# Small matmuls of four token mixers regrouped by array tile: RWKV scores, solved blocks and samples, HGRN2 outputs, attention heads in pairs

## The chip, the cores and the metric

The kernel runs on one core of a Trainium2 chip. The metric is the device time of one execution in microseconds (us). TensorE (PE in the profile) multiplies, VectorE (DVE), ScalarE (ACT) and GpSimd (POOL) do the elementwise work, SyncE (SP) issues most transfers. Each engine works through an instruction list of its own, whose order is fixed when the program is built.

## The reference, cut to what matters

Two layers of a decoder trunk in float32, on 288 token columns: a prompt of 256 tokens and 8 samples of 4 tokens each. A layer is

```python
u = RMSNorm(x); cols = u @ W_in            # 1024 wide, projections of four mixers and four gate blocks
o_A = RG-LRU(...)                          # convolution, gates, linear recurrence
o_B = RWKV-7(...)                          # 4 heads of 64, matrix state
o_C = HGRN2(...)                           # 4 heads, 128 features a head, values of 64
o_D = attention(...)                       # 4 heads of 64, dilated windows, 1024 cached positions for samples
x += W_o(sum_n sigmoid(G_n) * (o_n @ P_n))
x += W_down(gelu(conv3(v @ W_gate)) * (v @ W_up)),  v = RMSNorm(x)
```

The parts that the change touches are these. RWKV-7 steps a state `s = s*w + (s a) b' + v k'` and reads `s r`; HGRN2 sums `att = q k exp(decay)` within and between chunks of 64 and multiplies by the values; the attention takes a softmax of masked scores and multiplies by the values.

## The kernel before, in words

Features lie on partitions, tokens on columns. Two kinds of matmul share TensorE.

**The stream.** Every large weight is fetched in chunks of 512 KB (`chunk`, L320), split by ACT and DVE into two float32r parts `h` and `l`, and multiplied with the split activations (`prod`, L330): three products of 128x288 per 128x128 block of weights. These are the rows `pm<-tp,h`, `pm<-tp,l`, `pm<-y,h` and so on. `unit` (L1374) queues nine of them and then calls `mix`.

**The mixers.** Each mixer is a generator: RG-LRU (`branch_a`), RWKV (`branch_b`, L521), HGRN2 (`branch_c`, L914, two instances of a head pair each) and the attention (`branch_d`, L1135). `mix` (L1356) lets the mixers whose gap (`GAP`, L140) has passed go on by one `yield`, at most four of them in a slot. The small matmuls that they queue thus stand between the stream's products. `ORDER` (L147) sets the order of projections and gates. What stands in the program in this way is then put into one list per engine by a scheduler.

Small products are mostly float32 (a float32 product leaves two records in the trace, so x16 of them is 8 products; a streamed float32r product leaves one). A product may use part of the 128x128 array: 64 contracted rows in either row half, 64 or 32 output columns in a column half or quarter. "Tile" below is such a part, written rows x columns.

PSUM has three sets of banks (`BANKS`, L138): 3 `pm` for the stream, 2 `xb` for RWKV (and the attention's samples), 3 `xc` for HGRN2 and the attention. A name such as `xb<-b,kb` is out<-in.

The places that the change touches:

- `scores(h, a, q)` in RWKV (L730): for one head parity h (row half h) the four 128x128 score blocks of two head pairs and two chunks, into one `xb` bank. It is called eight times a layer: for `ab` (L737) and for the three matrices of `zz` (L814).
- `samples()` in RWKV (L625): the samples' small problem, with heads stacked on partitions in quarters.
- The loop over two chunks (L828 to 883): the solved product `u = X rr` (with `Y` a 64x64 tile and `Z` a 128x64 tile), the new state, and the outputs.
- HGRN2's outputs (L1067 to 1075): per head five products, of 64-row and 128-row tiles by turns.
- The attention's prompt heads (L1289 to 1327): scores, softmax, three transposes, three products with the values, one head after another.

## Time and profile before

| | us |
|---|---|
| time, median of 3 runs | 1227.33 (1226.59 to 1227.88) |
| the profiled execution: span | 1226.4 |
| TensorE busy in it | 1191.4 (97%) |
| VectorE busy | 854.3 (70%) |
| ScalarE busy | 612.2 (50%) |
| GpSimd busy | 551.5 (45%) |

The profiled execution's own time is shown as its span alone; the page has no other figure for it, and the span lies 0.9 us under the median of the runs. A row of the timeline gives the start of a run of like records, its length to the last modelled end, and the engine, line, operation, names, tile (rows*columns of the array), output and count. Matmuls overlap, so the distance from a start to the next start is what a run takes from the engine. Idle time before a run stands in brackets with what ended it. The windows give busy time per engine in a stretch of the span, and `PEclk`, the clock that TensorE was granted (1.00 is 2.4 GHz, 0.50 is 1.2 GHz).

### The profile page before, as it was taken

What the parts mean: (1) busy time and instruction counts of PE and PEld (TensorE: products, weight loads), DVE (VectorE), ACT (ScalarE), POOL (GpSimd) and SP (SyncE); (2) the same over time, 40 slices, a digit from 0 to 9 for tenths busy, and PEclk for the clock granted to TensorE, in tenths of its full rate; (3) what the DMA queues carried; (4) which work ended last, traced back from release to release, by engine and by line L of the source; (5) the groups of instructions that cost most, each with busy time, mean ns of one, the idle gap of its engine ahead of it and who ended that gap; (6) DMA issues with size and microseconds to landing.
All of it is one profiled execution on the core that took longest, in us unless ns stands there. A gap on an engine that the chain in (4) does not pass through costs nothing.

```text
span 1226.4 us, 26434 instructions
## 1 busy us (share of the span) xinstructions
PE 1191.4 (97%) x10596; PEld 1118.1 (91%) x10596; DVE 854.3 (70%) x1383; ACT 612.2 (50%) x1044; POOL 551.5 (45%) x862
## 2 busy tenths in 40 slices
PE   7988999999999999999998999999999999999997
PEld 6987788997899999999998978899889999999997
DVE  7897757576468888875568887575655878888543
ACT  5776446454345444443367844464543454444432
POOL 3745537240335666642228337352312636656322
PEclk9998999999999999999998989999999999999999
DMA  7344137248545555555543432543665455555552
GB/s 253 126 133 140 53 122 249 87 141 293 188 155 166 175 167 170 160 177 169 161 161 123 139 104 86 190 166 104 210 244 194 145 160 173 166 166 161 180 164 82
DMA packets 64042, 196.33 MB, mean 160 GB/s; under 512 B 8416, under 2 KB 12640, under 8 KB 63920
## 3 DMA queue, kind: packets, MB, share of 16 engines
q1 hardware_dynamic: 61872, 189.56, 47.1%
q0 software_dynamic: 1328, 4.33, 1.1%
q8 instruction: 83, 1.36, 0.4%
q10 hardware_dynamic: 720, 0.76, 0.2%
q14 instruction: 39, 0.32, 0.1%
HBM read 187.08 MB, written 6.49 MB: 158 GB/s over the span
## 4 chain that ended last, share of the span: by engine, by line
PE 83%; DVE 6%; POOL 4%; ACT 2%; issue 2%; DMA 2%; SPq 0%; DVEq 0%; ACTq 0%; POOLq 0%
PE pm L179 48%; PE xc L179 26%; PE xb L179 8%; POOL b L193 1%; DVE l L193 1%; DMA c<-in_vc 1%; POOL a L193 1%; DVE c L193 1%; DMA w<-in_w 1%; PE xc L182 1%; DVE c L956 1%; DVE c L202 1%; POOL b L200 1%; DVE b L196 0%; ACT h L185 0%
## 5 line engine op out<-in xcount | busy, mean ns | idle before, releaser
L179 PE MATMUL pm<-tp,h 128*128 128x288 f32 x2880 | 606.4, 302 | 5.9 <-DVE a L193 3.8
L185 ACT ACTIVATE h<-w 128x1024 fp32r<-128x1024 f32 x299 | 316.1, 1059 | 398.3 <-issue 211.9
L179 PEld LDWEIGHTS pm<-tp,h 128*128 128x128 f32 x2880 | 471.5, 191 | 16.7 <-ACT c L185 4.2
L193 DVE TENSOR_TENSOR l<-w,h 128x1024 fp32r<-128x1024 f32 x299 | 383.4, 1282 | 112.5 <-ACT h L185 111.3
L179 PE MATMUL pm<-tp,l 128*128 128x288 f32 x1440 | 431.8, 300 | 2.5 <-DVE l L193 2.5
L179 PEld LDWEIGHTS pm<-tp,l 128*128 128x128 f32 x1440 | 275.2, 191 | 7.6 <-DVE l L193 4.0
L179 PE MATMUL xc<-tp,h 128*128 128x288 f32 x896 | 183.9, 296 | 1.6 <-ACT tp L185 0.9
L179 PEld LDWEIGHTS xc<-tp,h 128*128 128x128 f32 x896 | 144.7, 188 | 3.3 <-ACT tp L185 1.3
L179 PE MATMUL xc<-tp,l 128*128 128x288 f32 x448 | 132.3, 295 | 0.0
L193 POOL TENSOR_TENSOR tmp<-a,rs 128x256 f32<-128x256 f32 x96 | 74.9, 800 | 72.5 <-ACT a L185 72.5
L193 POOL TENSOR_TENSOR tp<-tp,th 128x288 f32<-128x288 f32 x48 | 50.1, 1060 | 105.5 <-DVE th L196 105.5
L196 DVE SCALAR_TENSOR_TENSOR a<-a,pv,a 128x304 f32<-128x304 f32 (+2 forms) x112 | 84.2, 752 | 7.2 <-ACT a L185 5.5
L179 PEld LDWEIGHTS xc<-tp,l 128*128 128x128 f32 x448 | 84.3, 188 | 0.4 <-DVE l L193 0.4
L193 POOL TENSOR_TENSOR tmp<-x 128x288 f32<-128x288 f32 x28 | 28.3, 1009 | 108.0 <-DVE x L193 107.7
L193 DVE TENSOR_TENSOR th<-pm,rs 128x288 f32<-128x288 f32 x64 | 29.1, 455 | 60.9 <-PE pm L179 60.5
L193 POOL TENSOR_TENSOR c<-c 128x512 f32<-128x512 f32 (+2 forms) x32 | 37.2, 1178 | 47.1 <-PE xc L179 41.4
L193 DVE TENSOR_TENSOR tmp<-pm,tmp 128x288 f32<-128x288 f32 x48 | 22.0, 458 | 39.1 <-POOL tmp L193 39.0
L185 ACT ACT_TABLE_LOAD x34 | 43.6, 1283 | 0.6
L179 PE MATMUL pm<-y,h 128*128 128x288 f32 x192 | 41.1, 302 | 0.0
L185 ACT ACTIVATE c<-c 128x256 f32<-128x256 f32 (+2 forms) x68 | 30.7, 499 | 16.0 <-POOL c L193 15.1
L185 ACT ACTIVATE a<-a 128x304 f32<-128x304 f32 (+2 forms) x76 | 33.8, 446 | 9.9 <-DVE a L196 6.6
L193 DVE TENSOR_TENSOR c<-c,c 128x256 f32<-128x256 f32 (+2 forms) x56 | 34.9, 660 | 3.5 <-ACT c L185 3.3
(304 smaller groups left out, 1922.7 us busy)
## 6 DMA issues: line engine op xcount, KB each, us to landing
w<-in_wf SPq DMA_DIRECT2D x96, 512.0 KB, 3.6
w<-in_wg SPq DMA_DIRECT2D x64, 512.0 KB, 3.8
w<-in_w SPq DMA_DIRECT2D x59, 512.0 KB, 3.5
w<-in_wd SPq DMA_DIRECT2D x48, 512.0 KB, 3.5
c<-in_kc SPq DMA_DIRECT2D x32, 320.0 KB, 5.7
c<-in_vc SPq DMA_DIRECT2D x32, 320.0 KB, 5.0
w<-in_wb SPq DMA_DIRECT2D x16, 512.0 KB, 3.7
w<-in_wo SPq DMA_DIRECT2D x16, 512.0 KB, 3.5
```

Source lines behind the costliest of these rows:

```text
L179: nc.tensor.matmul(o, a, b, start=start, stop=stop)
L182: nc.tensor.transpose(o, i, ident)
L185: S.activation(o, i, f, **kw)
L193: e.tensor_tensor(o, a, b, op)
L196: V.scalar_tensor_tensor(o, a, s, b, op0, op1)
L200: (e or V).tensor_scalar(o, a, s1, None, op0)
L202: (e or V).tensor_scalar(o, a, s1, s2, op0, op1)
L956: V.tensor_tensor_scan(pr(b, h), C("crst", 0, 256), pr(f, h), 0.0, MUL, ADD)
```

## The change

The order in which the mixers' small products are queued is altered, and some of them are put on other tiles. The arithmetic is the same sum in another grouping.

- **RWKV scores.** `scores(a, q)` fills the banks of both head parities at once, the parity being the innermost loop. `ab` and the three matrices of `zz` are taken from such pairs.
- **RWKV samples.** The products for `b` and `k` over head pairs get a bank and a place of their own. The products with the cached state take `at` and `rt` directly, four products of a 64x32 tile each, in place of two of a 64x64 tile on a gathered copy. The addition of `sar` to `rr` is done by DVE in place of four products with the identity. The output products are grouped by operand, and all lie on 32x64 tiles.
- **RWKV solved blocks.** `Y` gets zeros in its lower half (a GpSimd memset), and the product of the upper blocks uses all 128 rows. State and output products are queued with the head innermost.
- **HGRN2 outputs.** `ato` holds the diagonal and the cross block of a 128-token chunk (with zeros in the third quadrant), so that a head has three products of N=128 on 128x64 tiles; the two heads of a pair alternate.
- **Attention.** Prompt heads are taken in pairs: both heads' scores, both softmaxes, six transposes, six products with the values, the heads alternating.
- **RWKV's small rank products.** `pa` is queued right behind `pw`.

The core of the diff (comments that the new file drops are left out):

```diff
+            pw, pa = X("xb")[:, :N], X("xb")[:, :N]
+            first = mm(pw, lora[0:64, 0, f], wa[0:64])
+            with tc.issue_after(first.ins):
+                mm(pa, lora[64:128, 0, f], wa[64:128])
...
-            p, pk = X("xb"), X("xb")
+            p = X("xb")
             for n, (a, q) in enumerate(((bt, at), (kt, at), (bt, rt), (kt, rt))):
                 for h in range(4):
                     mm(p[hr(h), n * NS:(n + 1) * NS], a[h // 2][rows(h), sc], q[h // 2][rows(h), sc])
             for h in range(4):
-                i, z = h // 2, 64 * (h % 2)
-                one = ident[rows(h), rows(h)]
-                mm(p[hr(h), P:P + 64], v[i][rows(h), sc], one)
-                mm(pk[z:z + NS, i * 64:i * 64 + 64], bt[i][rows(h), sc], one)
-                mm(pk[z + NS:z + 64, i * 64:i * 64 + 64], kt[i][rows(h), sc], one)
+                mm(p[hr(h), P:P + 64], v[h // 2][rows(h), sc], ident[rows(h), rows(h)])
             yield
...
-            act(stk[:, :P], pk[:, :P], AF.Copy)
             vh = stk[:, P:192]
             act(vh, p[:, P:192], AF.Copy)
+            p = X("xb")
+            for h in range(4):
+                i, z = h // 2, 64 * (h % 2)
+                one = ident[rows(h), rows(h)]
+                mm(p[z:z + NS, i * 64:i * 64 + 64], bt[i][rows(h), sc], one)
+                mm(p[z + NS:z + 64, i * 64:i * 64 + 64], kt[i][rows(h), sc], one)
+            act(stk[:, :P], p[:, :P], AF.Copy)
...
-            ar = R([P, 2, 2, NS], "sm")
-            for i in range(2):
-                G.tensor_copy(ar[:, i, 0], at[i][:, sc])
-                G.tensor_copy(ar[:, i, 1], rt[i][:, sc])
             sar = []
-            for i in range(2):
+            for src in (at, rt):
                 p = X("xb")
-                for z in range(2):
-                    mm(p[rows(z)], ar[rows(z), i].rearrange("p w t -> p (w t)"), s0[i][rows(z)].rearrange("p b v -> p (b v)"))
+                for h in range(4):
+                    mm(p[hr(h)], src[h // 2][rows(h), sc], s0[h // 2][rows(h)].rearrange("p b v -> p (b v)"))
...
             for h in range(4):
-                z = 64 * (h % 2)
-                mm(p[hr(h), :64], zs[hr(h), 0], vh[hr(h)], start=True, stop=False)
-                mm(p[hr(h), :64], ident[rows(h), z:z + NS], sar[h // 2][rows(h)], start=False, stop=True)
+                mm(p[hr(h), :64], zs[hr(h), 0], vh[hr(h)])
...
-            act(rr, p[:, :64], AF.Copy)
+            tt(V, rr, p[:, :64], sar[0], ADD)
...
-            ps_ = [X("xb"), X("xb")]
-            for h in range(4):
-                o = ps_[h // 2][rows(h), :NS]
-                mm(o, u[hr(h)], zs[hr(h), 1], start=True, stop=False)
-                mm(o, vh[hr(h)], zs[hr(h), 2], start=False, stop=False)
-                z = 64 * (h % 2) + NS
-                mm(o, sar[h // 2][rows(h)], ident[rows(h), z:z + NS], start=False, stop=True)
-            yield
             for i in range(2):
-                act(py[i][:, sc], ps_[i][:, :NS], AF.Copy)
+                p = X("xb")
+                for n, a in enumerate((vh, sar[1], u)):
+                    for h in (2 * i, 2 * i + 1):
+                        b = (zs[hr(h), 2], ident[hr(h), hr(h)], zs[hr(h), 1])[n]
+                        mm(p[rows(h), :NS], a[hr(h)], b, start=n == 0, stop=n == 2)
+                act(py[i][:, sc], p[:, :NS], AF.Copy)
+            yield
...
-        def scores(h, a, q):
-            p = X("xb")
+        def scores(a, q):
+            ps_ = [X("xb"), X("xb")]
             for i in range(2):
                 for c in range(2):
                     z, s = 2 * i + c, slice(c * P, c * P + P)
-                    mm(p[:, z * P:(z + 1) * P], a[i][rows(h), s], q[i][rows(h), s])
-            return p.rearrange("p (a b) -> p a b", a=4)
+                    for h in range(2):
+                        mm(ps_[h][:, z * P:(z + 1) * P], a[i][rows(h), s], q[i][rows(h), s])
+            return [p.rearrange("p (a b) -> p a b", a=4) for p in ps_]
         ab, abo = (R([P, 8, 64], "kb") for _ in range(2))
-        for h in range(2):
-            p, o = scores(h, bt, at), slice(4 * h, 4 * h + 4)
-            yield
+        sab = scores(bt, at)
+        yield
+        for h, p in enumerate(sab):
+            o = slice(4 * h, 4 * h + 4)
             for r in (0, 64):
                 act(ab[r:r + 32, o], p[r:r + 32, :, r:r + 64], AF.Copy)
                 act(ab[r + 32:r + 64, o, 0:32], p[r + 32:r + 64, :, r + 32:r + 64], AF.Copy)
             act(abo[0:64, o], p[0:64, :, 64:128], AF.Copy)
...
+        G.memset(Y[64:128], 0.0)
+        zz = [[], []]
+        for a, q, mk in ((kt, at, "us"), (bt, rt, "ui"), (kt, rt, "ui")):
+            pair = scores(a, q)
+            yield
+            for h, p in enumerate(pair):
                 z = R([P, 4, P], "kb")
                 G.memset(z, 0.0)
-                p = scores(h, a, q)
-                yield
                 V.copy_predicated(z, Mn(mk, 4), p)
-                row.append(z)
-            zz.append(row)
+                zz[h].append(z)
...
-                    mm(p[0:64, o], Y[0:64, z], rr[0:64, o])
+                    mm(p[0:64, o], Y[:, z], rr[:, o])
                     mm(p[64:128, o], Z[:, z], rr[:, o])
...
-                for h in range(2):
-                    o, tc_ = p[rows(h), i * 64:i * 64 + 64], slice(c * P + 64 * h, c * P + 64 * h + 64)
-                    mm(o, tk[i][0][:, tc_], u[:, i, hc(h)], start=True, stop=False)
-                    mm(o, tk[i][1][:, tc_], tk[i][2][:, tc_], start=False, stop=True)
-            yield
+                for m in (1, 0):
+                    for h in range(2):
+                        o, tc_ = p[rows(h), i * 64:i * 64 + 64], slice(c * P + 64 * h, c * P + 64 * h + 64)
+                        mm(o, tk[i][m][:, tc_], tk[i][2][:, tc_] if m else u[:, i, hc(h)], start=m == 1, stop=m == 0)
+            yield
...
-                for h in range(2):
-                    o, tc_ = p[rows(h), i * P:(i + 1) * P], slice(c * P + 64 * h, c * P + 64 * h + 64)
-                    mm(o, u[:, i, hc(h)], zz[h][1][:, 2 * i + c], start=c == 0, stop=False)
-                    mm(o, tk[i][2][:, tc_], zz[h][2][:, 2 * i + c], start=False, stop=True)
+                for m in (2, 1):
+                    for h in range(2):
+                        o, tc_ = p[rows(h), i * P:(i + 1) * P], slice(c * P + 64 * h, c * P + 64 * h + 64)
+                        mm(o, tk[i][2][:, tc_] if m == 2 else u[:, i, hc(h)], zz[h][m][:, 2 * i + c],
+                           start=c == 0 and m == 2, stop=m == 1)
             yield
...
-        ato = R([P, 4, 64], "kc")
-        act(ato[0:64], p[0:64, :256].rearrange("p (z m) -> p z m", z=4), AF.Copy)
-        G.tensor_copy(ato[64:128], att[64:128])
+        ato = R([P, 4, P], "kc")
+        G.memset(ato[64:128, :, 0:64], 0.0)
+        G.tensor_copy(ato[0:64, :, 0:64], att[0:64])
+        G.tensor_copy(ato[64:128, :, 64:P], att[64:128])
+        act(ato[0:64, :, 64:P], p[0:64, :256].rearrange("p (z m) -> p z m", z=4), AF.Copy)
...
-        for h in range(2):
-            r = rows(h)
-            v0, v1 = vt[:, h * 64:(h + 1) * 64], vt[:, P + h * 64:P + (h + 1) * 64]
-            mm(p[r, 0:64], v0[0:64], att[0:64, h])
-            mm(p[r, 64:P], v0, ato[:, h])
-            mm(p[r, P:TP], v0, a01[:, h], start=True, stop=False)
-            mm(p[r, P:P + 64], v1[0:64], att[0:64, 2 + h], start=False, stop=False)
-            mm(p[r, P + 64:TP], v1, ato[:, 2 + h], start=False, stop=True)
+        for o_, c, m, start, stop in ((0, 0, ato, True, True), (P, 0, a01, True, False), (P, 1, ato, False, True)):
+            for h in range(2):
+                mm(p[rows(h), o_:o_ + P], vt[:, c * P + h * 64:c * P + (h + 1) * 64], m[:, 2 * c + h], start=start, stop=stop)
...
-        def scores(h):
-            p, i = X("xc")[:, :384], h // 2
+        def scores(i):
+            ps_ = [X("xc")[:, :384] for _ in range(2)]
             for lo, q0, w in ((0, 0, P), (P, P, TP)):
-                mm(p[:, lo:lo + w], qs[rows(h), i, q0:q0 + P], ks_[rows(h), i, :w])
-            return p
+                for z, p in enumerate(ps_):
+                    mm(p[:, lo:lo + w], qs[rows(z), i, q0:q0 + P], ks_[rows(z), i, :w])
+            return ps_
...
-        e = softmax(p)
-        for h in range(4):
-            if h < 3:
-                p = scores(h + 1)
-            yield
-            pe = X("xc")
-            for n in range(3):
-                tr(pe[:, n * P:(n + 1) * P], e[:, n])
-            yield
-            t = R([P, 3, P], "kc")
-            act(fl(t), pe[:, :384], AF.Copy)
-            if h < 3:
-                e = softmax(p)
-            yield
-            hc = slice(64 * h, 64 * h + 64)
-            mm(y[rows(h), h // 2, 0:P], vt[0][:, hc], t[:, 0])
-            mm(y[rows(h), h // 2, P:TP], vt[0][:, hc], t[:, 1], start=True, stop=False)
-            mm(y[rows(h), h // 2, P:TP], vt[1][:, hc], t[:, 2], start=False, stop=True)
+        for i in range(2):
+            es = [softmax(q_) for q_ in p]
+            yield
+            pes = [X("xc") for _ in range(2)]
+            for e, pe in zip(es, pes):
+                for n in range(3):
+                    tr(pe[:, n * P:(n + 1) * P], e[:, n])
+            yield
+            ts_ = []
+            for pe in pes:
+                ts_.append(R([P, 3, P], "kc"))
+                act(fl(ts_[-1]), pe[:, :384], AF.Copy)
+            if i == 0:
+                p = scores(1)
+            yield
+            for o_, c, n in ((0, 0, 0), (P, 0, 1), (P, 1, 2)):
+                for z, t in enumerate(ts_):
+                    mm(y[rows(z), i, o_:o_ + P], vt[c][:, (2 * i + z) * 64:(2 * i + z + 1) * 64], t[:, n],
+                       start=n < 2, stop=n != 1)
```

Three places show what the scheduler made of it, all on PE in the first layer.

HGRN2's outputs, first head of pair 0, before, behind the products of the pair's state. `kc_1860` is `att`, `kc_2325` and `kc_2360` are `ato` and `a01` (each name is the operand that streams; the values are `a_2399`); a row reads out<-moving,held. The other head's last four and the second pair's ten follow in the same manner.

```order
L179 MATMUL xb_1561<-b_1170,kb_1029 32x32 x32
L179 MATMUL xc_2457<-a_2413,kc_2455 128x64 x4
L179 MATMUL xc_2465<-kc_1860,a_2399 64x64
L179 MATMUL xc_2465<-kc_2325,a_2399 64x64
L179 MATMUL xc_2465<-kc_2360,a_2399 64x128
L179 MATMUL xc_2465<-kc_1860,a_2399 64x64
L179 MATMUL xc_2465<-kc_2325,a_2399 64x64
L179 MATMUL xc_2465<-kc_1860,a_2399 64x64
```

The same head pair and then the other one, after:

```order
L179 MATMUL xb_1591<-kb_1589,b_1123 32x32 x32
L179 MATMUL xc_2493<-a_2446,kc_2491 128x64 x4
L179 MATMUL xc_2501<-kc_2351,a_2432 64x128 x2
L179 MATMUL xc_2501<-kc_2390,a_2432 64x128 x2
L179 MATMUL xc_2501<-kc_2351,a_2432 64x128 x2
L179 MATMUL xc_2520<-kc_2380,a_2446 64x128 x2
L179 MATMUL xc_2520<-kc_2421,a_2446 64x128 x2
L179 MATMUL xc_2520<-kc_2380,a_2446 64x128
L179 MATMUL xb_1643<-b_1124,kb_1029 32x32 x32
L179 MATMUL xc_2520<-kc_2380,a_2446 64x128
```

A head's five products, which go from a 64x64 to a 128x64 tile and back, became three on a 128x64 tile, the pair's two heads in two column halves (x2). Eleven of the twelve products of both pairs now stand in a row, and the last behind 32 products of RWKV's doubling.

RWKV's scores for two of the `zz` matrices, before (`xb_2218` and `xb_2304` are the banks of two matrices of the same parity, row half 0):

```order
L179 MATMUL pm_2992<-tp_101,l_2996 128x288
L179 MATMUL xb_2218<-b_912,b_910 128x128 x2
L179 MATMUL xb_2218<-b_975,b_973 128x128 x2
L179 MATMUL xb_2304<-b_912,b_913 128x128 x2
L179 MATMUL xb_2304<-b_975,b_976 128x128 x2
L179 MATMUL xc_2718<-a_2720,blk 128x288
L179 MATMUL pm_2992<-tp_103,h_2995 128x288
```

After, `xb_2051` is the second parity (row half 64) of one matrix and `xb_2133` the first parity (row half 0) of the next:

```order
L179 MATMUL pm_2968<-tp_93,l_2972 128x288
L179 MATMUL xb_2051<-b_797,b_913 128x128 x2
L179 MATMUL xb_2051<-b_838,b_976 128x128 x2
L179 MATMUL xb_2133<-b_912,b_910 128x128 x2
L179 MATMUL xb_2133<-b_975,b_973 128x128 x2
L179 MATMUL xc_2724<-a_2725,blk 128x288
L179 MATMUL xc_2724<-a_2726,blk 128x288
```

The two parities of one matrix don't alternate product by product; four of one row half stand ahead of four of the other. The run is again eight products long.

The output products of RWKV's samples, before, behind HGRN2's levels (`zs` the scores, `sm_1243` is `u`, `b_1095` holds `vh`, `sm_1186` is `sar`, with `cst` the identity). The three of the first head are shown; nine like them follow for the other heads:

```order
L179 MATMUL xc_2102<-c_179 64x64 x8
L179 MATMUL xc_2134<-c_178 64x64 x8
L179 MATMUL xb_1261<-zs,sm_1243 64x32
L179 MATMUL xb_1261<-zs,b_1095 64x32
L179 MATMUL xb_1261<-cst,sm_1186 64x32
```

After, the first of the two groups, with what stands behind it:

```order
L179 MATMUL pm_2083<-tp_98,h_2086 128x288
L179 MATMUL xb_1265<-zs,b_1091 64x32 x2
L179 MATMUL xb_1265<-cst,sm_1217 64x32 x2
L179 MATMUL xb_1265<-zs,sm_1247 64x32 x2
L179 MATMUL xc_2100<-c_2061 32x32 x2
L179 MATMUL pm_2083<-tp_97,l_2087 128x288
```

Twelve products in one stretch became two groups of six, each in a stretch of its own among the stream's products, and `u` comes last in a group in place of first.

## Rows read from the trace of the kernel before

**Rows 1.** The page, its first part: busy time of each engine.

```profile
PE 1191.4 (97%) x10596; PEld 1118.1 (91%) x10596; DVE 854.3 (70%) x1383; ACT 612.2 (50%) x1044; POOL 551.5 (45%) x862
```

**Rows 2.** Windows: stretch, length, then busy us per engine, PEclk, DMA share, GB/s.

```profile
100.00:150.00 50.00, 47.08 (x465) 39.06 (x464) 38.85 (x75) 23.23 (x55) 26.57 (x31) 0.93 0.25 78
200.00:250.00 50.00, 50.00 (x421) 45.88 (x421) 28.69 (x48) 25.85 (x45) 19.98 (x26) 1.00 0.40 128
400.00:450.00 50.00, 50.00 (x381) 50.00 (x380) 42.16 (x66) 22.96 (x33) 32.28 (x59) 1.00 0.53 170
```

**Rows 3.** Windows around TensorE's waits, same columns.

```profile
105.70:110.96 5.26, 2.34 (x26) 1.84 (x24) 5.26 (x17) 2.82 (x5) 3.62 (x6) 0.92 0.12 47
111.00:116.60 5.60, 5.60 (x23) 5.60 (x24) 4.83 (x11) 0.19 (x1) 3.36 (x6) 0.50 0.56 177
125.00:161.00 36.00, 33.84 (x448) 26.27 (x447) 29.44 (x50) 16.09 (x37) 20.47 (x27) 1.00 0.23 75
662.20:666.70 4.50, 1.10 (x6) 0.56 (x4) 4.39 (x9) 0.85 (x3) 3.31 (x7) 0.98 0.45 140
666.70:673.40 6.70, 6.67 (x25) 5.91 (x26) 5.38 (x13) 5.62 (x15) 4.06 (x11) 0.51 0.38 136
```

**Rows 4.** Timeline of PE, HGRN2 outputs of both head pairs, layer 0.

```profile
176.95 2.56 PE L179 MATMUL xc<-kc,a 64*64 64x64 f32 x20
179.44 0.75 PE L179 MATMUL xb<-kb,b 32*32 32x32 f32 x64
180.12 2.57 PE L179 MATMUL xc<-kc,a 64*64 64x64 f32 x20
```

**Rows 5.** Timeline of PE, a solved product, then state and output products, layer 0.

```profile
227.13 2.12 PE L179 MATMUL xb<-b,kb 64*64 64x64 f32 x16
229.18 0.40 PE L179 MATMUL pm<-tp,l 128*128 128x288 f32 x1
...
232.45 0.73 PE L179 MATMUL xb<-b,b 128*64 128x64 f32 x16
232.97 1.10 PE L179 MATMUL xb<-kb,b 128*64 128x128 f32 x16
233.99 0.40 PE L179 MATMUL pm<-tp,h 128*128 128x288 f32 x1
```

**Rows 6.** Timeline of PE, RWKV scores of two matrices, one parity.

```profile
211.85 2.05 PE L179 MATMUL xb<-b,b 64*128 64x128 f32 x16
213.82 0.40 PE L179 MATMUL xc<-a,blk 128*128 128x288 f32 x1
```

**Rows 7.** Timeline of PE, attention: scores of two heads, values, scores of one.

```profile
277.24 0.93 PE L179 MATMUL xc<-kc,kc 64*128 64x128 f32 x8
278.10 1.28 PE L179 MATMUL xb<-c,qb 128*32 128x512 f32 x14
...
288.56 0.87 PE L179 MATMUL xc<-kc,a 128*64 128x128 f32 x6
289.36 0.92 PE L179 MATMUL xc<-kc,kc 64*128 64x128 f32 x4
290.21 1.06 PE L179 MATMUL xb<-c,qb 128*32 128x512 f32 x8
```

**Rows 8.** Timeline of PE, RWKV samples: one product alone, then the output stage.

```profile
130.34 0.29 PE L179 MATMUL pm<-tp,l 128*128 128x288 f32 x1
130.56 0.29 PE L179 MATMUL xb<-b,zs 32*32 32x64 f32 x2
130.78 0.53 PE L179 MATMUL pm<-tp,h 128*128 128x288 f32 x2
...
140.08 0.30 PE L179 MATMUL xb<-zs,sm 32*64 32x32 f32 x2
140.43 0.30 PE L179 MATMUL xb<-cst,sm 64*64 64x32 f32 x2
...
142.37 0.45 PE L179 MATMUL xc<-c 128*64 128x64 f32 x8
```

More of the change, by code (lines that the diff above doesn't have):

```diff
@@ L178, in mm @@
     def mm(o, a, b, start=True, stop=True):
-        nc.tensor.matmul(o, a, b, start=start, stop=stop)
+        return nc.tensor.matmul(o, a, b, start=start, stop=stop)
     def tr(o, i):
@@ L702, in samples @@
                 G.tensor_copy(uv[z:z + NS, h // 2], u[hr(h)])
-            ps_ = [X("xb"), X("xb")]
-            for h in range(4):
-                o = ps_[h // 2][rows(h), :NS]
-                mm(o, u[hr(h)], zs[hr(h), 1], start=True, stop=False)
-                mm(o, vh[hr(h)], zs[hr(h), 2], start=False, stop=False)
-                z = 64 * (h % 2) + NS
-                mm(o, sar[h // 2][rows(h)], ident[rows(h), z:z + NS], start=False, stop=True)
+            for i in range(2):
[5 more added lines that the diff above has]
+                act(py[i][:, sc], p[:, :NS], AF.Copy)
             yield
-            for i in range(2):
-                act(py[i][:, sc], ps_[i][:, :NS], AF.Copy)
             for i in range(2):
@@ L812, in branch_b @@
         act(Z[0:64], p[0:64], AF.Copy)
-        zz = []
-        for h in range(2):
-            row = []
-            for a, q, mk in ((kt, at, "us"), (bt, rt, "ui"), (kt, rt, "ui")):
+        G.memset(Y[64:128], 0.0)
[4 more added lines that the diff above has]
+            for h, p in enumerate(pair):
                 z = R([P, 4, P], "kb")
                 G.memset(z, 0.0)
-                p = scores(h, a, q)
-                yield
                 V.copy_predicated(z, Mn(mk, 4), p)
-                row.append(z)
-            zz.append(row)
+                zz[h].append(z)
         def hc(h):
@@ L1067, in branch_c @@
         p = X("xc")
-        for h in range(2):
-            r = rows(h)
-            v0, v1 = vt[:, h * 64:(h + 1) * 64], vt[:, P + h * 64:P + (h + 1) * 64]
-            mm(p[r, 0:64], v0[0:64], att[0:64, h])
-            mm(p[r, 64:P], v0, ato[:, h])
-            mm(p[r, P:TP], v0, a01[:, h], start=True, stop=False)
-            mm(p[r, P:P + 64], v1[0:64], att[0:64, 2 + h], start=False, stop=False)
-            mm(p[r, P + 64:TP], v1, ato[:, 2 + h], start=False, stop=True)
+        for o_, c, m, start, stop in ((0, 0, ato, True, True), (P, 0, a01, True, False), (P, 1, ato, False, True)):
+            for h in range(2):
+                mm(p[rows(h), o_:o_ + P], vt[:, c * P + h * 64:c * P + (h + 1) * 64], m[:, 2 * c + h], start=start, stop=stop)
         yield
@@ L1309, in branch_d @@
         yield
[L1310 to L1313 removed]
+        for i in range(2):
+            es = [softmax(q_) for q_ in p]
             yield
[L1315 to L1317 removed]
+            pes = [X("xc") for _ in range(2)]
+            for e, pe in zip(es, pes):
+                for n in range(3):
+                    tr(pe[:, n * P:(n + 1) * P], e[:, n])
             yield
[L1319 to L1322 removed]
+            ts_ = []
[4 more added lines that the diff above has]
+                p = scores(1)
             yield
[L1324 to L1327 removed]
+            for o_, c, n in ((0, 0, 0), (P, 0, 1), (P, 1, 2)):
+                for z, t in enumerate(ts_):
+                    mm(y[rows(z), i, o_:o_ + P], vt[c][:, (2 * i + z) * 64:(2 * i + z + 1) * 64], t[:, n],
+                       start=n < 2, stop=n != 1)
         yield
```

4 lines of the change are left out of this document (removed).

## The prediction

> **What bounds the kernel now.** I read the page's busy times first, then TensorE in windows, then the stretches around its waits, then the timeline of each place that the change touches. TensorE is busy 1191.4 us, 97% of the span [rows 1]. In windows of 50 us it is full where RWKV's solved part runs (50.00 at 200 to 250) as in a stretch of pure stream (50.00 at 400 to 450) [rows 2]. The stream row also gives the price of a streamed matmul: 381 in 50 us, 0.131 us each. So in most of the kernel every us that a mixer's small products take from TensorE is a us of the result, and an engine beside it that gets work for nothing costs nothing as long as TensorE doesn't wait for it.
>
> Three stretches are otherwise [rows 3]. At 105.70 to 110.96 TensorE is busy for 2.34 of 5.26 us, and then 23 matmuls take 5.60 us at a granted clock of 0.50, the 1.2 GHz level, where 23 x 0.131 would be 3.0: the idle time was 2.9 us, the slow clock after it 2.6 more. At 125 to 161 it is busy for 33.84 of 36.00, while DVE is busy for 29.44: there HGRN2's levels on DVE are nearly the bound. At 662.20 to 666.70 it is idle for 3.4 us, and the next 25 matmuls take 6.70 us at 0.51 in place of 3.3, another 3.4 lost: such an event costs 6.8 us in all.
>
> **The change part by part.** All prices are for one layer; the second layer has the same places with the same counts, so the sum is doubled. Of a pair of starts the distance counts, since ends are modelled.
>
> HGRN2's outputs: 10 products take 2.49 us (176.95 to 179.44), the other pair's the like at 180.12, 5.0 in all [rows 4]. That is 0.25 a product. In their place come twelve of N=128 on 128x64 tiles, two column halves by turns. The nearest row is RWKV's outputs, the same tile and N: 8 products in 1.02 us (232.97 to 233.99), 0.128 each [rows 5]. Twelve are 1.53, and the twelfth, behind RWKV's quads, is one change of tile more, some 0.15 (below): 1.7. Gain 3.3.
>
> Solved product: 8 products of 64x64 and 128x64 by turns take 2.05 us (227.13 to 229.18). With all on 128x64 the nearest row is the state's 8 products of the same tile and N: 0.52 (232.45 to 232.97) [rows 5]. Gain 1.5, two such a layer: 3.0. The memset of `Y` is on GpSimd, which is busy 45% [rows 1] and has the scores' time to do it; without that cover the first solved product would wait for it.
>
> The new order of state and output products: those 0.52 and 1.02 us for 8 products [rows 5] are measured with two products of a column half behind one another. One half alone costs 0.80 for three (288.56 to 289.36) [rows 7], 0.27 each, against 0.128. The halves thus overlap already, and alternating them gains 0.
>
> RWKV scores: two runs of 8 products take 1.97 us each (211.85 to 213.82 is one) [rows 6], 0.25 a product, all on one row half. After the change such a run has four of one row half and four of the other. The row for that is the attention's: two heads, whose scores lie on the two row halves, take 0.86 us (277.24 to 278.10), one head alone 0.85 (289.36 to 290.21) [rows 7], though they were queued head after head. So the second half is free, and a run falls to 0.98: gain 1.0 each, 2.0 a layer. Bounds: 0, if four in a row are too many to look past, and 2.0. I take 2.0, since the row has the same tile. The other stretches of scores keep their four products.
>
> The Trainium skill, "TensorE: Matmul & The Clock Gate", Part 3 ("The mechanism"), speaks against this: it says that matmuls start and end strictly in the order in which they are queued. By that rule only the last of the first four could run beside the first of the second four, 0.25 of each run, and the sum would be worse by 1.5 a layer, 3.0 us in all. The row at 277.24 doesn't agree, since by the rule the two heads' products, queued as they are, would take longer than one head's. The Trainium skill, "TensorEngine Tiling (Array Packing)", "Key Properties", says that a change of tiling mode drains the engine; the dear products of rows 4 and rows 8 agree.
>
> Attention: values cost 0.80 for one head [rows 7], 3.2 for four. Six products of a pair, two column halves by turns, are 6 x 0.128, so 1.5 for both pairs: gain 1.7. The second pair's scores stand apart by row half in the new order and keep 0.85 each: 0. Both softmaxes now lie between scores and transposes; what is queued meanwhile is the stream, so a later step costs nothing.
>
> RWKV samples: the output stage takes 2.29 us (140.08 to 142.37) for 12 products whose tile changes for every third [rows 8], 0.19 each, where 0.065 is the price without changes (0.52 for 8, [rows 5]): a change costs 0.15 to 0.2. Without changes 12 x 0.065 are 0.8: gain 1.5. The `rr` products were 8 of changing tiles, about 8 x 0.19 = 1.5, and are 4, 0.3: gain 1.2. The products with the cached state go from two 64x64 to four 64x32 each; the attention's run at 278.10 has 7 products of 512 and 128 columns in four column quarters and takes 1.28 [rows 7], where one behind the other, at 0.27 per 128 columns, would be 4.3. So the quarters overlap: 0; bound: 1.07 more for each of the two runs (512 columns at 0.27 per 128) if only two do. `rr` now waits for DVE in place of ACT. Queued behind that on TensorE is the product `u`, and behind it the stream, but the step stands several slots later, so 0.
>
> What is added: the two orders have 55 stretches of small products in a layer before and 61 after (the samples' outputs and the `b`, `k` products stand alone now, HGRN2's levels come in smaller pieces). One stretch of a single product costs 0.44 between two streamed starts (130.34 to 130.78) in place of 0.13 [rows 8], 0.31. Six are 1.9. About seven pieces are odd, each with a product that finds no partner, 0.13: 0.9. Together 2.8 lost.
>
> Sum: -3.3 - 3.0 - 2.0 - 1.7 - 2.7 + 2.8 = -9.9 a layer.
>
> What comes back: the samples' 2.7 lie almost wholly at 120 to 145, in the stretch in which TensorE already waits for HGRN2's chain on DVE (2.2 idle of 36, DVE 82% busy) [rows 3]. That chain isn't shortened, so TensorE, with less to do, waits for it longer. Between 0 and 2.7 is given back. I take 2.2, as the chain is nearly full there. What is saved later, from 161 on, meets a full TensorE and stays. Left: -7.7 a layer, -15.4 in all. On the profiled span of 1226.4 that is 1211.0; the runs' median is 0.9 above the span, so **about 1212 us**.
>
> **The rivals.**
>
> 1. Scores don't overlap four deep. The row at 277.24 has two products a head, and four need a longer look ahead. If nothing overlaps, all of the 2.0 is lost; if only the pair at the border does (the fourth product of one half with the first of the other, 0.25), 1.5: 3 to 4 us more in two layers, 1215 to 1216. Against it: the row above. By the rule of the Trainium skill, "TensorE: Matmul & The Clock Gate", Part 3, it would be the second of these.
>
> 2. HGRN2's chain takes more than it got. RWKV's solver starts earlier in the new order, so its small copies on DVE and ACT stand among the levels' steps. If DVE, 29.44 of 36 busy, falls behind by 2 to 3 us a layer more, and each new wait is followed by some of the half clock of [rows 3], 4 to 10 us come back: 1216 to 1222. For it speaks the wait in the window 125 to 161; against it that the list of DVE hardly changes and ACT is busy for less than half of it.
>
> 3. Slower: the two `xb` banks. `scores` now fills both at once, and nothing of RWKV or the samples can enter TensorE's queue until DVE or ACT has emptied one. TensorE works in order, so the whole stream stands behind a product that waits for a bank. Four pairs of scores a layer give eight such chances. If one becomes a wait like that at 662.20, it costs 6.8 us with its slow clock [rows 3]; two are covered by the saving (13.6 of 15.4), three (20.4) give 1232 or more. Against it: TensorE has no wait at all at 200 to 250, where DVE is busy for 28.69 and ACT for 25.85 of 50 [rows 2], and the scheduler has put other work between.
>
> 4. The change doesn't do what it says: the alternation is not there (the scores' order shows that it isn't product by product), and the products with zeros added cost what the short ones did. Then the sums for HGRN2 and solved blocks, 6.3 a layer, shrink to the changes of tile alone, and the added stretches (2.8) eat most of the rest: 1221 to 1228. Against it: the rows that I priced with have these very tiles.
>
> **How the numbers follow.** A measurement of this kernel can tell 0.2%, 2.5 us, from no change. Forecast (1206 to 1215) 0.53; rival 1 0.14; rival 2 0.16; rival 3 0.08; rival 4 0.09, half of it within 0.2%. Faster: 0.53 + 0.14 + 0.16 + 0.045 = 0.875, say 0.87; same 0.05; slower 0.08. The range: at the low end nothing is given back (-19.8: 1207.5), and the wait at 105.70 swallows one us a layer of the new stretches: 1205. At the high end rival 2 in full: 1222. That leaves out rival 3 and half of rival 4, and with a part of the forecast's own misses about 0.2.
>
> **What would show it.** Right: the solved run at about 0.5 us in place of 2.05; twelve HGRN2 products in 1.5 to 1.8; a run of eight scores near 1.0; the samples' six outputs near 0.4; TensorE's busy time lower by some 18, its idle time higher by 2 to 5, around 125 to 161 and the same place in the second layer. Wrong: scores at 1.9; new idle time between 200 and 335 or a granted clock of 0.50 there; a longer wait before HGRN2's levels; products with the cached state above 1.1 us a run.

## The result: 1211.1 us, a ratio of 0.987, and the profile after

The changed kernel takes 1211.1 us (median of 4 runs, 1209.15 to 1212.02) where the kernel before takes 1226.96 (4 runs): a ratio of 0.9872, interval 0.9858 to 0.9886. The forecast was 1212, in a range of 1205 to 1222. The profiled execution took 1212.02 us, its span 1210.2, 16.2 less than the span before.

The page of the changed kernel, first part, to be held against [rows 1]:

```profile
PE 1172.3 (97%) x10564; PEld 1102.2 (91%) x10564; DVE 848.4 (70%) x1385; ACT 611.3 (51%) x1042; POOL 552.8 (46%) x864
```

TensorE is busy for 19.1 us less, at the same share of 97%, and idle for 2.9 us more (37.9 in place of 35.0). Nothing else moved much: DVE is 5.9 us less busy, ACT and GpSimd are level. So the gain is TensorE's, as the sum assumed. The timeline of PE at the places of [rows 4], [rows 5] and [rows 8] (start, length, names, tile, output, records):

```profile
133.34 0.30 PE L179 MATMUL xb<-zs,b 32*64 32x32 f32 x4
133.47 0.28 PE L179 MATMUL xb<-cst,sm 32*64 32x32 f32 x4
133.59 0.28 PE L179 MATMUL xb<-zs,sm 32*64 32x32 f32 x4
133.80 0.26 PE L179 MATMUL xc<-c 128*32 128x32 f32 x4
...
170.97 1.52 PE L179 MATMUL xc<-kc,a 128*64 128x128 f32 x22
172.42 0.75 PE L179 MATMUL xb<-b,kb 32*32 32x32 f32 x64
173.11 0.43 PE L179 MATMUL xc<-kc,a 128*64 128x128 f32 x2
173.47 1.04 PE L179 MATMUL xc<-kc,c 128*32 128x512 f32 x3
...
218.52 0.69 PE L179 MATMUL xb<-b,kb 128*64 128x64 f32 x16
219.03 0.29 PE L179 MATMUL xb<-b,b 128*64 128x64 f32 x4
219.25 0.40 PE L179 MATMUL pm<-tp,h 128*128 128x288 f32 x1
...
283.06 0.88 PE L179 MATMUL xc<-kc,a 128*64 128x128 f32 x12
283.87 0.41 PE L179 MATMUL xb<-c,qb 128*32 128x128 f32 x2
```

Eleven of HGRN2's twelve products take 1.45 us (170.97 to 172.42), the twelfth 0.36: 1.81 in place of 5.0. The eight solved products take 0.51 in place of 2.05. Six output products of the samples take 0.46, so twelve 0.92 in place of 2.29. Six products of the attention with the values take 0.81 where three took 0.80.

Two places are not as forecast. RWKV's scores, against [rows 6], and the fourth run of them:

```profile
199.45 1.71 PE L179 MATMUL xb<-b,b 64*128 64x128 f32 x16
201.09 0.40 PE L179 MATMUL xc<-a,blk 128*128 128x288 f32 x1
...
210.30 0.42 PE L179 MATMUL pm<-tp,h 128*128 128x288 f32 x2
211.72 1.16 PE L179 MATMUL xb<-b,b 64*128 64x128 f32 x8 [1.00 <-DVE kb L820]
212.81 1.47 PE L179 MATMUL xb<-b,kb 128*128 128x64 f32 x8
```

The run of eight products takes 1.64 us where 1.97 stood and 0.98 was forecast, and the run at 211.72 first waits 1.00 us for DVE's masked copy out of the bank. The windows around TensorE's waits, against [rows 3]; the last line is the first window in the kernel before:

```profile
105.00:115.00 10.00, 7.63 (x49) 6.89 (x48) 10.00 (x29) 3.81 (x7) 4.59 (x4) 0.83 0.25 78
140.00:146.00 6.00, 4.47 (x60) 2.83 (x58) 6.00 (x9) 3.61 (x9) 3.47 (x4) 1.00 0.02 4
211.00:217.00 6.00, 5.28 (x29) 5.16 (x30) 3.76 (x7) 2.27 (x5) 2.66 (x3) 0.72 0.53 173
125.00:161.00 36.00, 33.84 (x580) 28.07 (x581) 30.63 (x51) 16.12 (x37) 26.52 (x37) 1.00 0.24 79
105.00:115.00 10.00, 7.08 (x48) 6.58 (x47) 10.00 (x26) 3.34 (x7) 7.72 (x11) 0.76 0.29 97
```

Behind the wait at 211.72 the clock falls (0.72 in the window). At 140 to 146 TensorE is idle for 1.5 us while DVE is full (6.00 of 6.00): it waits for HGRN2's levels. These are the products `xc<-c` and `xc<-c,c` that build `att` within chunks, one size of block after the other, each from operands that DVE has just multiplied. Yet over 125 to 161 TensorE is busy for 33.84 of 36.00 us, as it was before. At 105 to 115 there is one wait in place of two, and the clock is 0.83, where it was 0.76 in the same window before. The waits of PE in the first layer (what waited, for what; us in all, times, the longest), after and then before:

```profile
PE pm L179 <- DVE l L193: 2.1, 1, 2.1
PE xc L179 <- DVE c L193: 2.1, 3, 1.1
PE xb L179 <- DVE kb L820: 1.0, 1, 1.0
```
```profile
PE xc L179 <- DVE c L193: 2.1, 2, 1.1
PE pm L179 <- DVE a L193: 1.9, 1, 1.9
PE pm L179 <- DVE l L193: 1.0, 1, 1.0
```

After, the first is the one that is left at 105 to 115, the second are three waits for the levels, the third is the one for the bank. The wait for `DVE a` is gone, and the wait for the levels is no longer than before in this layer; in the second layer it rose from 0.6 to 2.1.

**The account of TensorE's time.** I took the starts of all TensorE records from RWKV's first scores to the last sample products of the attention and charged the distance from each start to the next to the later record's group, with its wait if it had one; a streamed matmul behind a small one was charged 0.13 and the rest went to the small group. By this rule the stream's wait for `DVE l`, which comes behind a product of the levels, stands in the levels' row: 1.0 / 0.6 us of it before, 2.1 / 2.1 after. "Half clock" is a granted clock of 0.50. All of it is worked out from the two traces. In us, first layer / second layer:

| group | before | after | forecast of the step, a layer | measured |
|---|---|---|---|---|
| values (HGRN2 and attention) | 8.8 / 8.8 | 4.0 / 4.0 | -5.0 | -4.8 |
| solved products | 4.3 / 4.3 | 1.4 / 1.4 | -3.0 | -2.9 |
| RWKV scores | 8.8 / 8.8 | 9.3 / 9.2 | -2.0 | +0.5 |
| RWKV samples | 9.0 / 7.8 | 5.4 / 4.6 | -2.7 | -3.4 |
| HGRN2's levels | 16.9 / 15.6 | 20.1 / 20.1 | | +3.9 |
| attention's scores and transposes | 3.8 / 3.8 | 4.5 / 4.5 | 0 | +0.7 |
| other small products | 47.6 / 47.1 | 48.4 / 48.3 | | +1.0 |
| stream: waits and half clock | 11.6 / 11.9 | 9.9 / 8.6 | | -2.5 |
| stream at full clock | 135.1 / 140.2 | 135.1 / 140.2 | | 0 |
| all | 245.9 / 248.2 | 238.0 / 241.0 | -7.7 | -7.6 |

Four rows together (levels, the attention's scores and transposes, other small products, waits and half clock) are what the prediction put down as stretches (+2.8) and time given back (+2.2): +5.0 forecast, +3.1 measured. With the wait for `DVE l` put to the stream, the levels rose by 2.5 and the stream's waits and half clock fell by 1.2. Of the 2.5, only 0.7 is longer waiting; the rest goes with the levels' products, which stand in 24 runs a layer where they stood in 18. 15.1 of the 16.2 us of the span lie in these two stretches; the rest came ahead of RWKV's first scores, where the two programs hardly differ (these four runs of the kernel before differ by 2.7 among themselves, and all its runs lie from 1220.54 to 1227.99). RWKV's small rank products, which the change also moves and the prediction gave no term, stand there: they cost 2.4 and 3.0 us in the two layers, before and after.

### The profile page after: what moved, and what is told of

It is laid out like the page before. It is cut to its first block, busy times and chain, and to the rows that moved or that the text cites. A ratio compares the mean times of both kernels' runs of the same rounds, so it can differ in the third digit from the quotient of the medians.

```text
span 1210.2 us, 26415 instructions
## 1 busy us (share of the span) xinstructions
PE 1172.3 (97%) x10564; PEld 1102.2 (91%) x10564; DVE 848.4 (70%) x1385; ACT 611.3 (51%) x1042; POOL 552.8 (46%) x864
## 4 chain that ended last, share of the span: by engine, by line
PE 74%; DVE 9%; POOL 6%; ACT 4%; DMA 4%; issue 3%; DVEq 0%; SPq 0%; ACTq 0%; POOLq 0%
PE pm L179 43%; PE xc L179 24%; PE xb L179 5%; DVE c L193 2%; DVE l L193 2%; POOL b L193 1%; ACT L185 1%; DMA c<-in_vc 1%; DMA w<-in_w 1%; DVE b L196 1%; POOL a L193 1%; ACT a L185 1%; ACT h L185 1%; PE xc L182 1%; DMA kc<-in_cs 1%
## 5 line engine op out<-in xcount | busy, mean ns | idle before, releaser
L185 ACT ACTIVATE a<-a 128x304 f32<-128x304 f32 (+2 forms) x76 | 33.6, 445 | 13.6 <-DVE a L196 7.8
L193 DVE TENSOR_TENSOR c<-c,c 128x256 f32<-128x256 f32 (+2 forms) x56 | 38.8, 734 | 1.7 <-ACT c L185 1.4
```

Source lines behind the costliest of these rows:

```text
L185: S.activation(o, i, f, **kw)
L193: e.tensor_tensor(o, a, b, op)
```

## The experiments

Each ratio is against runs of the kernel before on the same chip, with its interval.

**Parts alone on the kernel before.** First HGRN2's outputs:

```diff
+        ato = R([P, 4, P], "kc")
...
-            mm(p[r, 0:64], v0[0:64], att[0:64, h])
-            mm(p[r, 64:P], v0, ato[:, h])
...
+                mm(p[rows(h), o_:o_ + P], vt[:, c * P + h * 64:c * P + (h + 1) * 64], m[:, 2 * c + h], start=start, stop=stop)
```

> The kernel before, with HGRN2's outputs of the change alone. The prediction's step: 3.3 us a layer, all kept, since TensorE is full there: 6.6 us, about 1220.5. Rival: GpSimd's memset and copies for the larger operand make the outputs wait, and half of it is lost: 1223 to 1224.

1220.8 us, ratio 0.9955 (0.9939 to 0.9972): -5.5, between 3.4 and 7.5. In the account the values fall from 8.8 to 5.3 in either layer, 3.5 against the 3.3 of the step. The gain is kept for the most part.

The solved product alone:

```diff
+        G.memset(Y[64:128], 0.0)
...
-                    mm(p[0:64, o], Y[0:64, z], rr[0:64, o])
+                    mm(p[0:64, o], Y[:, z], rr[:, o])
```

> The kernel before, with the solved product on all 128 rows (Y with a lower half of zeros) and nothing else. The prediction's step: 1.5 us for each of four products, 5.8 to 6.0 in all, about 1221. Rival: the zeros are contracted at the price of the array's rows and a product takes as long as before: 1227.

1219.4 us, 0.9948 (0.9933 to 0.9963): -6.4. The account has solved products at 1.4 in place of 4.3. The step holds: the run of eight, four of which now have twice the rows, half of them zeros, costs a quarter. A row of the kernel before tells what of this is the change of tile, eight 64x64 products that all lie on one tile:

```profile
202.18 1.14 PE L179 MATMUL xb<-kb,kb 64*64 64x64 f32 x16
203.26 0.40 PE L179 MATMUL pm<-tp,l 128*128 128x288 f32 x1
```

They take 1.08 us. So by an estimate from these rows, about 1.0 of the 1.54 us saved is the changes of tile (2.05 less 1.08). The other 0.6 (1.08 less 0.51) is that the two column halves, now tiles of one kind, overlap.

The attention's pairs alone, and the changed kernel without them (the same lines the other way):

```diff
-        def scores(h):
+        def scores(i):
...
-        for h in range(4):
+        for i in range(2):
+            es = [softmax(q_) for q_ in p]
```

> The kernel before, with the attention's heads in pairs and nothing else. The prediction's step: 1.7 us a layer from the values, 0 from the rest: 3.4, about 1223.5. Rival, from the changed kernel's trace: scores and transposes of the second pair, cut in pieces, take 0.7 a layer back: 2.0, about 1225.

> The changed kernel without the attention's part (heads one after another as before). If the parts add, it is slower than the changed kernel by what the attention alone gains on the kernel before: 2 to 3.4 us, 1213 to 1214.5. If the pairs collide with the other parts, it is level with it or faster: 1211 or less.

Alone 1224.5 us, 0.9991 (0.9979 to 1.0002): at most 2.6 gained, not the 3.4 of the step. The changed kernel without the pairs takes 1210.5, 0.9877 (0.9860 to 0.9893), level with it. The values fall by 1.5 a layer, of 1.7 forecast, and scores and transposes take 0.7 back, as the rival has it. The part is worth little.

The samples' part alone, all of the diff's lines in `samples()`:

```diff
-            p, pk = X("xb"), X("xb")
+            p = X("xb")
...
-            for i in range(2):
+            for src in (at, rt):
...
+                for n, a in enumerate((vh, sar[1], u)):
```

> The kernel before, with the RWKV samples' part of the change alone. The prediction's step: 2.7 us a layer saved, a stretch more for b and k (0.3), 2.2 given back to HGRN2's chain: about 1226. Theory A, from the changed kernel's trace: little is given back, since the waits at 105.70 to 110.96 get shorter with DVE's work in another order and fewer streamed matmuls run at the half clock behind them: 3 to 5 us a layer, 1217 to 1221.

1238.0 us, 1.0096 (1.0070 to 1.0122): 12 us slower, which neither case expected. The samples' own products fell as they should, from 9.0 / 7.8 to 5.6 / 5.8. What rose is HGRN2's levels (19.0 / 19.3), the other small products (49.6 / 49.5, with 82 stretches of small products where 75 stood), the stream's waits and half clock (13.8 / 12.9), and the attention's scores and transposes (5.8 / 4.7, where 3.8 stood, with a wait of 2.0 us for the softmax in the first layer). The timeline of PE in this kernel, idle time in brackets, and the window around it:

```profile
148.79 0.69 PE L179 MATMUL xc<-c 128*64 128x64 f32 x16 [0.97 <-DVE c L193]
150.66 0.54 PE L179 MATMUL xc<-c 128*64 128x64 f32 x6 [1.18 <-DVE kc L967]
...
153.82 1.12 PE L179 MATMUL xc<-c 128*64 128x64 f32 x16 [0.77 <-DVE c L193]
```
```profile
145.00:160.00 15.00, 12.08 (x239) 10.02 (x236) 13.95 (x21) 5.57 (x11) 7.92 (x12) 0.77 0.22 73
```

TensorE comes to the levels three times before DVE is done with their operands (DVE is busy for 13.95 of 15 us), and the clock falls to 0.77 in the window. This is what the prediction's second rival describes: waits for the levels, with half clock behind them.

**The scores.** The changed kernel with the scores taken per row half, as before:

```diff
-        sab = scores(bt, at)
+        for h in range(2):
+            p, o = scores(h, bt, at), slice(4 * h, 4 * h + 4)
...
-            pair = scores(a, q)
+                p = scores(h, a, q)
```

> The changed kernel, with RWKV's scores taken per row half as before. Theory A: filling both banks at once costs more than the border overlap gives, since the fourth run of scores waits 1.0 us for DVE's masked copy (211.72) and half clock follows: without it the kernel is 2 to 5 us below the changed one (1206 to 1209), and TensorE doesn't wait between 195 and 225. Rival B: the scores' part is a gain as forecast, and without it the kernel is 1 to 4 us slower (1212 to 1215).

1227.9 us, 1.0010 (0.9991 to 1.0029): all of the gain is gone, and neither theory said so. The scores themselves are cheaper than in the changed kernel (8.9 against 9.3 a layer), so it isn't the overlap that pays. What rises is around them: the stream's waits and half clock by 4.2 / 4.6, the attention's scores and transposes by 4.3 / 1.5, the solved products by 0.8. The waits of PE in the first layer:

```profile
PE xc L182 <- DVE kc L200: 2.0, 1, 2.0
PE pm L179 <- DVE a L193: 2.0, 1, 2.0
...
PE xc L179 <- DVE kc L970: 1.2, 1, 1.2
...
PE xc L179 <- DVE c L193: 1.6, 2, 1.0
```

The wait for `DVE a` at the place of [rows 3], 105.70, is there again, the attention's transposes wait 2.0 us for the softmax (`kc` L200), and HGRN2's levels 2.8 in all. The wait of 1.9 to 2.0 us for `DVE a` stands in each of the seven kernels with scores per row half (the one before, the HGRN2, solved, attention, samples and bank parts alone, and this one). In the seven with pairs it is gone, or 0.7 (in twos, below).

Samples and pairs together on the kernel before, without the other three parts:

```diff
-            p, pk = X("xb"), X("xb")
+            p = X("xb")
...
-        def scores(h, a, q):
+        def scores(a, q):
```

> The kernel before, with the samples' part and the paired scores together (HGRN2, solved product and attention as before). The samples alone made it 12 us slower, and the changed kernel without the pairs is 17 us slower than with them. If the parts add, this kernel is the changed one less the gains of the other three alone (5.3 + 6.6 + 1.5): 1224 to 1225, so the pairs take back what the samples cost, by their place in the order and not by overlap. Rival: the samples' cost belongs to their meeting with the old scores alone, and with the pairs their own tiles pay in full: 1218 to 1220.

1224.2 us, 0.9995 (0.9983 to 1.0007). The parts add, as the expectation's first case has it: the pairs take back what the samples cost. With HGRN2's outputs (5.5), the solved product (6.4), the attention's pairs (1.1) and these two (0.6), the parts give 13.6 of the 15.7 us by their ratios, and the intervals cover the rest. Of the 12.7 us between the spans of the two kernels (1236.1 and 1223.4), 7.3 are TensorE's busy time (which holds matmuls at half clock) and 5.4 its idle time:

```profile
PE 1192.3 (96%) x10596; PEld 1116.8 (90%) x10596; DVE 855.8 (69%) x1385; ACT 617.0 (50%) x1046; POOL 539.8 (44%) x854
```
```profile
PE 1185.0 (97%) x10596; PEld 1110.2 (91%) x10596; DVE 853.0 (70%) x1385; ACT 614.6 (50%) x1046; POOL 546.8 (45%) x854
```

The pairs alone, without the samples' one bank at a time, were not tried: the samples of before hold both `xb` banks at once, as a pair of scores does.

Which half of the samples' part costs? One bank at a time (the `b` and `k` products in one of their own, the outputs of a head pair after the other's), on the old tiles, on the kernel before:

```diff
-            ps_ = [X("xb"), X("xb")]
-            for h in range(4):
-                o = ps_[h // 2][rows(h), :NS]
+            for i in range(2):
+                p = X("xb")
+                for h in (2 * i, 2 * i + 1):
+                    o = p[rows(h), :NS]
```

> The kernel before, with the samples' products on their old tiles, but with one bank at a time: the b and k products in a bank and stretch of their own, the outputs of a head pair one bank after the other. Theory A: the 12 us that the samples' part costs alone come from this, through the order of the work on TensorE and DVE: 1233 to 1240. Rival B: they come from the products' new tiles and the shorter way to them: 1226 to 1229 here.

1227.9 us, 1.0026 (1.0012 to 1.0040): 3 us of the 12, so rival B. The rest comes with the new tiles, which do save time on TensorE. The same old tiles in the changed kernel:

```diff
-                    mm(p[hr(h)], src[h // 2][rows(h), sc], s0[h // 2][rows(h)].rearrange("p b v -> p (b v)"))
...
+                    mm(p[rows(z)], ar[rows(z), i].rearrange("p w t -> p (w t)"), s0[i][rows(z)].rearrange("p b v -> p (b v)"))
...
-            tt(V, rr, p[:, :64], sar[0], ADD)
+            act(rr, p[:, :64], AF.Copy)
```

> The changed kernel, with the samples' products on the tiles of before (gathered operands for the cached state, rr with the identity, outputs head by head), but one bank at a time as in the change. Theory A: the tiles are worth what they save on TensorE, 3.2 to 3.7 us a layer: 1217 to 1218.5. Rival B, the prediction's step: most of that is given back as waiting for HGRN2's levels: 1211 to 1214.

1214.2 us, 0.9909 (0.9892 to 0.9927), so the tiles gain about 3 to 4.5 us there (0.9909 less 0.9872 is 0.0037). The samples' groups cost 8.6 / 7.6 with the old tiles and 5.4 / 4.6 with the new, 3.1 a layer; HGRN2's levels cost 16.4 with the old and 20.1 with the new, the other small products 50.0 and 48.4. So some 1 to 1.5 of 3.1 is given back, and the time lies between theories A and B, at the edge of B. One and the same edit is worth 3 to 4.5 us here and costs some 9 (12 less 3) on the kernel before.

**Can the row halves overlap?** The changed kernel with the scores held in alternating order (the lines shown), and in twos (`for i in range(2) for h in (1, 0) for z in (2 * i, 2 * i + 1)` in place of that list):

```diff
-                    for h in range(2):
-                        mm(ps_[h][:, z * P:(z + 1) * P], a[i][rows(h), s], q[i][rows(h), s])
+            for h, z in [(h, z) for z in range(4) for h in (1, 0)]:
...
+                    with tc.issue_after(last.ins):
+                        last = mm(o, x, y)
```

> The changed kernel, with RWKV's scores held in the order row half 64, row half 0, product by product. Theory A: TensorE looks only a few records past a busy row half, so four products of one half ahead of four of the other overlap at the border only (run of 8 in the changed kernel: 1.63 us, 199.45 to 201.09), and alternating them overlaps all of it: the stretch of 7 products falls to about 1.0 us, and the kernel is 1 to 3 us below the changed one (1208 to 1210). Rival B: float32 products of the two row halves share something, and a border is all that overlaps: the stretch of 7 takes about 1.4 to 1.6 us, and the kernel stands at 1211 to 1213, since one product of each pair is now in a stretch of its own (0.31 each).

> The changed kernel, with RWKV's scores held in the order two of row half 64, two of row half 0. The stretch of 6 products (0, 0, 64, 64, 0, 0) takes 1.5 us if nothing overlaps, about 1.0 if only one product at each of the two borders does, and about 0.8 if TensorE looks three records past a busy half, as the starts in the changed kernel's run at 199.45 suggest.

Alternating: 1202.2 us, 0.9804 (0.9782 to 0.9826), better than the changed kernel beyond both intervals. In twos: 1202.1 in one run. The timeline of PE, alternating and then in twos:

```profile
197.61 1.16 PE L179 MATMUL xb<-b,b 64*128 64x128 f32 x14
198.70 0.40 PE L179 MATMUL pm<-tp,h 128*128 128x288 f32 x1
```
```profile
198.41 1.16 PE L179 MATMUL xb<-b,b 64*128 64x128 f32 x12
199.49 0.40 PE L179 MATMUL pm<-tp,l 128*128 128x288 f32 x1
...
203.99 1.26 PE L179 MATMUL xb<-b,b 64*128 64x128 f32 x16
205.18 0.67 PE L179 MATMUL xc<-a,blk 128*128 128x288 f32 x3
```

Seven products take 1.09 us alternating; six in twos take 1.08, eight 1.19. Four of one half alone take 1.09 (212.81 less 211.72 in the changed kernel). So the second half is free by turns, and costs 0.10 for eight in twos; four ahead of four is too long, with 1.64. Theory A holds for the stretch, but not for the time: 9 us were gained, not 1 to 3. The six in twos can't tell how far TensorE looks: the expectation's 1.0, with one product overlapping at each border, already leaves no more than four of one half alone take. The eight can: in strict order they would take five products' time. Scores fell from 9.3 to 6.5 a layer. That is 2.7 of some 4.8 a layer (238.0 and 241.0 of the account became 232.3 and 237.1). More came from the row of HGRN2's levels, which fell from 20.1 to 15.4 / 15.6 (2.1 of it, or 2.0 in the second layer, is the stream's wait for `DVE l`), and some went back: 1.9 / 1.6 to the samples, 1.6 / 2.3 to the other small products. The waits of PE in the first layer show both: the wait for `DVE l` is gone, little is left of the wait for the levels (DVE c), and a new one of the samples for a bank stands first:

```profile
PE xb L179 <- ACT kb L185: 2.6, 1, 2.6
PE xb L179 <- DVE kb L824: 1.3, 1, 1.3
PE xc L179 <- DVE c L193: 0.6, 2, 0.3
```

Both orders are held by `issue_after`. Whether holding four ahead of four in the same way would bring some of what is gained beside the scores was not tried.

Last, alternating scores without the attention's pairs:

```diff
-        def scores(i):
+        def scores(h):
...
+                    with tc.issue_after(last.ins):
+                        last = mm(o, x, y)
```

> The changed kernel with alternating scores (1202.2) and without the attention's pairs. The attention's pairs gained 1.5 us on the kernel before and lost 0.6 in the changed kernel. If their scores and transposes in pieces (0.7 a layer) and the waits outweigh the values' gain: 1199 to 1202. If the values' 1.5 a layer counts where TensorE is full: 1203 to 1205.

1203.3 us, 0.9832 (0.9808 to 0.9856), level with alternating scores alone; the median lies in the second case's range. The best kernel of the study is the changed one with alternating scores, 9 us below it.

## Why the prediction was right

The time and the sum came out (-7.7 a layer forecast, -7.6 measured), but not every term, and the sum in part by luck.

- **Values and solved products**: -8.0 forecast, -7.7 measured, and either part alone on the kernel before gave its own again. The rows on the same tile and number of columns ([rows 5]) were the right price: this is what carried the forecast.
- **Alternating state and output products**: 0 forecast; by the starts in the two traces less than 0.1 a layer.
- **Scores**: the step that failed. It read from [rows 7] that the second row half is free whatever the order, and took 2.0. There the other head's products are two places behind; in a run of four and four they are four places behind. Measured: 0.33 saved a run, then 1.0 us of waiting for the bank and a slow clock: +0.5 a layer. Rival 1 had the first half of that, with its price (1.5 to 2.0 lost); rival 3 had the second, at one event of small size in each layer. The rule of the Trainium skill, "TensorE: Matmul & The Clock Gate", Part 3, gave 0.25 a run and came nearer than my reading. As a strict order it doesn't hold here: the eight products in twos, whose order the edit holds, would take five products' time in strict order, 1.34 (1.09 and 0.25), and took 1.19. [rows 7] points the same way, if its two heads were queued as the program has them.
- **Samples**: -2.7 forecast, -3.4 measured, with part of the wait for a bank in the first layer in it. The four column quarters of the products with the cached state cost no more, as forecast.
- **Stretches and time given back**: +5.0 forecast, +3.1 measured, but not for the reasons given. The prediction gave 2.2 a layer back as a longer wait for HGRN2's levels; that wait grew by 0.7 a layer (2.7 to 4.1 us in both). What grew is the time of the levels' own products, by 1.8. The two programs differ by about three stretches a layer in the traces, not by six. What the prediction hadn't got is a gain of 1.2 in the stream's waits and half clock: of the two waits at the place of [rows 3], 105.70 to 110.96, the one for `DVE a` is gone. By the runs it goes with the pairs of scores.
- So 2.5 missed on the scores and 0.3 on values and solved products were made good by 0.7 of the samples and 1.9 of the rest: wrong entries cancelled, and that is luck.
- **The rivals**: the chance of 0.08 for slower was put on the banks. The experiments show that a slower kernel was near, but by the second rival: the samples' part without the pairs is 12 us slower, with waits for HGRN2's levels and half clock behind them, which I had limited to 2 to 3 us a layer.

What stays open: why the pairs of scores take back what the samples' part costs. Shown is that they do (1238.0 and 1224.2; 1227.9 and 1211.1), and which waits go with it (those for `DVE a` in both cases, for the softmax in the second); which of the moved instructions decides was not separated, since the scheduler places all of them anew in each of these kernels.

## What to carry to other kernels

Small products are priced well by a row of the same tile and columns. Here a change of tile between them cost more than the rows of zeros that avoid it. Products on two halves of the array overlapped when they were queued by turns or in twos; write that order so that the scheduler can't undo it, and look at what it made of it. On a kernel with several interleaved chains the parts of a change are not worth what they are worth alone: here one edit cost 9 us or gained 4, depending on another.

## What the runs showed of the hardware

TensorE started a float32 product of the other row half about two places early: eight products take 1.97 us on one half, 1.64 as four and four and 1.19 in twos, and seven by turns take 1.09, as four of one half alone do. Products on 128x64 tiles in two column halves, some of them half zeros, cost 0.065 us each, where 64-row and 128-row products by turns cost 0.25 and 64-row products on one tile 0.135.
